# Low halves one step late, pooling products bank by bank, a traced background budget and results held in PSUM, in a two-layer encoder trunk

## The chip, the cores and the metric

The program runs on one core of one Trainium2 chip. The time is the device time of one execution in microseconds (us), from the host's measurement; the profile's span is the time from the first to the last instruction of one profiled execution. TensorE is called PE in the rows (PEld is its weight load), VectorE DVE, ScalarE ACT, GpSimd POOL and SyncE SP. SP issues nearly all loads.

## What is computed

Two post-norm layers over 256 tokens of width 1024, batch 1, all in float32. The part that matters, cut from the reference:

```python
proj = jnp.einsum('bsd,de->bse', x, w_in[i])          # 1024 -> 13824
(a_in, q_att, k_att, v_att, q_h, i_h, ff_h, fb_h, g_h, gate_raw) = jnp.split(proj, splits, axis=-1)
y_a = einsum(multiscale_pool(a_in, pool_w[i], pool_scale[i]), w_branch_a[i])
y_b = einsum(dilated_attention_mixer(q_att, k_att, v_att), w_branch_b[i])
y_c = einsum(hgrn2_bidirectional(q_h, i_h, ff_h, fb_h, g_h, ...), w_branch_c[i])
merged = gates[:, :, 0] * y_a + gates[:, :, 1] * y_b + gates[:, :, 2] * y_c
x1 = layer_norm(DEEPNORM_ALPHA * x + einsum(merged, w_out[i]), ...)
ffn = einsum(silu(einsum(x1, w_ffn_gate[i])) * einsum(x1, w_ffn_up[i]), w_ffn_down[i])
ple = einsum(p[i], w_ple_proj[i]) * sigmoid(einsum(x1, w_ple_gate[i]))
x = layer_norm(DEEPNORM_ALPHA * x1 + ffn + ple, ...)
```

`multiscale_pool` takes centred window means of four channel groups and multiplies each group of 256 channels by its own 256 x 256 matrix `pool_w` (the "pooling products"). HGRN is a gated linear recurrence, run forward and backward over 8 heads of 128, in blocks of time.

## The kernel before

**Weights in chunks.** All weights are read as 214 chunks of 1 MB, in the fixed order in which they are used (the list `chunks`, from L129). SP loads a chunk into a tile `raw`; ScalarE rounds it to its high half `whi` (L212); VectorE subtracts to get the low half `wlo` (L215) and then lets SP load the next chunk into a free `raw` tile. Activations are split in the same way, so a product is three matmuls: high by high, low by high, high by low (`mm3`, L320 to L322; `tok_part`, L369; `gemm_wide` for the FFN, L342). Each of `raw`, `whi`, `wlo` has three buffers, so a chunk can be split as soon as the products of the chunk three places earlier are done. `split_chunk` (L220) issues both halves of the next chunk; `split_later` issues the high half and returns the low half for the caller to place.

**Steps.** The main line is a row of steps, one for each chunk. Within a step TensorE multiplies the chunk into a PSUM bank (`gbank`, four of them, rows named g; `tbank`, four more, rows named t). A chunk of 256 columns (`gemm_cols`) is 48 matmuls of 256 columns; a chunk of the token-major kind (`tok_block`) is 24 matmuls of 512. At the end `step_end` (L309) first runs background work, then evacuates the bank (`then`), then calls `split_chunk`.

**Background.** HGRN (four tasks of two heads), attention (four tasks) and pooling (four tasks) run as Python generators that issue instructions in small pieces and yield the nanoseconds of VectorE time of each. `background` (L268) resumes them until a budget of 3000 is used up. A task that needs TensorE yields None and sleeps until `amid` (L262), which the main line calls in the middle of a chunk, lets it issue its small matmuls there. An HGRN task prepares, for each of two directions, decayed tiles in SBUF (rows named w: scans L486 to L494, reciprocals L499 and L501, products L503 to L539), then issues the products within blocks (the "diagonal", L552), with the second direction also those across blocks (L562, L569), copies them out and goes on to the output (L597 to L625). The tiles that feed the tasks (`half2k`, rows named h) are ten; `room` (L278) forces background work until enough are free. `live` counts the t banks in use and `held` the h tiles.

**Order.** The code sets the order on TensorE, VectorE and ScalarE itself (`manual_schedule`); each engine works through its instructions in that order. A row whose operands carry a wait stops all that stands behind it on that engine.

**Pooling products (from L996).** For each of the four groups one t bank is taken; for m = 0 and 1 the half m of the bank is multiplied (6 matmuls) and split at once into `ph` and `pl_` (L1009, which calls L389 on ScalarE and L390 on VectorE).

**Start and joints.** A few warming matmuls run while the first loads arrive (`spin`, L803), and the first chunk is split in four pieces. Where a layer norm passes the residual stream to the next products (`Handover`) the main line is written out by hand, with single `split_chunk` calls between parts of a chunk; the gate of the per-layer embedding (L1122, L1123 evacuate it) is such a place.

Of the kernel before, what the change touches and what calls it, by code (L numbers as in the profile page):

```python
# [78 lines left out]
def trunk(ctx: ExitStack, tc: tile.TileContext, x, p, w_in, pool_w, pool_scale, w_branch_a,  # L79
# [21 lines left out]
    def misc(shape, dt=F32):  # L101
        return tp.tile(shape, dt, tag="m", bufs=4, name="m")

# [36 lines left out]
    for l in range(DEPTH):  # L140
# [93 lines left out]
    def use_chunk():  # L234
        i = pos["use"]
        pos["use"] += 1
        return split.pop(i)
# [7 lines left out]
    asleep = set()  # L245
    gated = set()
    live = [0]
# [14 lines left out]
    def amid(width=3):  # L262
# [5 lines left out]
    def background(budget=3000, width=3):  # L268
        turn = 0
        while budget > 0:  # L270
# [5 lines left out]
            budget -= resume(t) or 0  # L276
# [32 lines left out]
    def step_end(then=None):  # L309


        background()
        if then is not None:
            then()
# [57 lines left out]
    def tok_block(act, evac, n=2):  # L372

        ps = [gbank(), gbank()]
        for i in range(n):
# [5 lines left out]
            step_end((lambda: [evac(t, ps[t]) for t in range(2)]) if i == n - 1 else None)  # L381
# [82 lines left out]
    def hgrn_task(l, hp, q, ff, kf, fb, kb, vt, gt, oh, ol):  # L464
# [4 lines left out]
        dg, across = None, []  # L469
# [9 lines left out]
        for d in range(2):  # L479
# [5 lines left out]
            if fwd:  # L485
                V.tensor_tensor_scan(out=Ct, data0=smask, data1=f0, initial=0.0, op0=ALU.max, op1=ALU.mult)  # L486
                yield 600
                V.tensor_tensor_scan(out=Rt[:, ::-1], data0=ft[:, 2:514][:, ::-1], data1=emask[:, ::-1],
                                     initial=0.0, op0=ALU.mult, op1=ALU.max)
            else:  # L490
                V.tensor_tensor_scan(out=Ct[:, ::-1], data0=emask[:, ::-1], data1=f0[:, ::-1],
                                     initial=0.0, op0=ALU.max, op1=ALU.mult)
                yield 600
                V.tensor_tensor_scan(out=Rt, data0=ft[:, 0:512], data1=smask, initial=0.0,  # L494
                                     op0=ALU.mult, op1=ALU.max)
            yield 600
# [3 lines left out]
            yield 1670  # L500
            V.reciprocal(out=k2[:, :, la, :], in_=C[:, :, la, :])  # L501
            yield 1670
# [15 lines left out]
            for L, blks, src, intra, own, far, fac in (  # L518
# [3 lines left out]
                for h in range(2):  # L522
                    b0 = blks[0]
                    cs = slice(h * S + 64 * b0, h * S + 64 * b0 + 192)
                    dst = L[:, h, 0:5:2, :].rearrange("p b (c u) -> p b c u", u=32)

                    def v(a):
                        return a[:, cs].rearrange("p (b c u) -> p b c u", c=2, u=32)
                    V.tensor_tensor(out=dst[:, :, own, :], in0=v(src)[:, :, own, :],
                                    in1=v(fac)[:, :, own, :], op=ALU.mult)  # L530
                    V.tensor_tensor(out=dst[:, :, far, :], in0=v(intra)[:, :, far, :],
                                    in1=tot[:, h, b0:b0 + 3, own, :].to_broadcast([P, 3, 32]), op=ALU.mult)
# [693 lines left out]
```

## Time and profile before

| what | value |
|---|---|
| runs, us | 1340.67, 1342.22, 3315.57; median 1342.22 |
| the profiled execution, us | 1341.88 |
| its span, us | 1339.6 |
| its mean granted TensorE clock | 0.983 |
| instructions in the span | 18867 |
| bytes read from HBM | 231.10 MB, 173 GB/s |

The span lies 2.3 us under the execution's own time. In the rows, a group's columns are busy time, mean ns of one, and the idle time of the engine before it with what ended it; a row of the waits gives total time, number and longest wait; a row of the timeline gives start, length, engine, line, operation, tiles and, in brackets, idle time of the engine before it and what ended it. The lengths of matmuls overlap, since they are pipelined: the pace is read from the starts.

The slices of the page, each a fortieth of the span, tenths of busy time and of granted clock:

```profile
PE   9999999999979999999999999999998999999997
DVE  5789897485536866665578999964745468666655
ACT  5444445454434455444254444454533344555541
PEclk9999999999979999999999999999999899999999
```

TensorE falls below 90% in the twelfth slice, with its clock, in the thirty-first, after which its clock falls, and in the last.

### The profile page before, as it was taken

To read this page: it belongs to the slowest core of one execution; us is meant where nothing else is said; L and a number is where in the kernel's file an instruction comes from. 1 tells how busy PE (TensorE), PEld (TensorE's weight loads), DVE (VectorE), ACT (ScalarE), POOL (GpSimd) and SP (SyncE) were. 2 spreads that over 40 slices of the span, in tenths; PEclk is the share of its full clock that TensorE was granted. 3 is DMA by queue.
4 is the path that set the end of the run, shared out by engine and by line. 5 is a ranking of instruction groups with operands and counts; after the bars stand their busy time and mean duration, and the time that the engine had idled before them with its cause. 6 is when DMAs were issued, how large, how long until landed. Compare 5 with 4: busy or idle time off the path is not lost.

```text
span 1339.6 us, 18867 instructions
## 1 busy us (share of the span) xinstructions
PE 1305.8 (97%) x7889; PEld 1152.9 (86%) x7889; DVE 907.6 (68%) x1233; ACT 615.0 (46%) x734; POOL 16.7 (1%) x24
## 2 busy tenths in 40 slices
PE   9999999999979999999999999999998999999997
PEld 7999999998868888888888998999987788888885
DVE  5789897485536866665578999964745468666655
ACT  5444445454434455444254444454533344555541
POOL 0000000000000000000000000000000000000000
PEclk9999999999979999999999999999999899999999
DMA  9555444445545475557555554444366364655570
GB/s 313 185 183 164 158 137 148 142 142 189 188 134 194 145 227 187 172 178 251 187 189 186 161 179 137 131 154 158 126 207 206 102 216 157 191 187 187 176 265 33
DMA packets 160292, 233.36 MB, mean 174 GB/s; under 512 B 3856, under 2 KB 108880, under 8 KB 160208
## 3 DMA queue, kind: packets, MB, share of 16 engines
q1 hardware_dynamic: 158512, 227.44, 51.5%
q10 hardware_dynamic: 1696, 4.72, 1.0%
q8 instruction: 62, 1.02, 0.3%
q14 instruction: 22, 0.18, 0.0%
HBM read 231.10 MB, written 1.05 MB: 173 GB/s over the span
## 4 chain that ended last, share of the span: by engine, by line
PE 74%; DVE 12%; ACT 8%; issue 5%; ACTq 0%; DVEq 0%
PE g L369 32%; PE g L320 11%; PE g L321 11%; PE g L322 11%; ACT whi L212 7%; DVE wlo L215 6%; DVE m L349 2%; DVE m L1163 1%; PE g L342 1%; PE t L569 1%; PE t L320 1%; PE t L552 1%; PE t L645 1%; PE t L408 1%; PE t L598 1%
## 5 line engine op out<-in xcount | busy, mean ns | idle before, releaser
L215 DVE TENSOR_TENSOR wlo<-raw,whi 128x2048 fp32r<-128x2048 f32 (+1 forms) x220 | 489.4, 2229 | 315.3 <-ACT whi L212 315.2
L212 ACT ACTIVATE whi<-raw 128x2048 fp32r<-128x2048 f32 (+1 forms) x220 | 409.2, 1864 | 178.3 <-PE g L369 107.3
L369 PE MATMUL g<-whi,xx 128*128 128x512 f32 x960 | 295.9, 395 | 1.1 <-ACT whi L212 0.8
L320 PE MATMUL g<-xx,whi 128*128 128x256 f32 x896 | 256.8, 287 | 0.0
L321 PE MATMUL g<-xx,whi 128*128 128x256 f32 x896 | 253.9, 283 | 0.0
L322 PE MATMUL g<-xx,wlo 128*128 128x256 f32 x896 | 253.7, 283 | 0.0
L369 PEld LDWEIGHTS g<-whi,xx 128*128 128x128 f32 x960 | 180.3, 191 | 38.0 <-ACT whi L212 2.2
L369 PE MATMUL g<-wlo,xx 128*128 128x512 f32 x480 | 182.7, 393 | 0.2
L320 PEld LDWEIGHTS g<-xx,whi 128*128 128x128 f32 x896 | 172.3, 192 | 0.7
L321 PEld LDWEIGHTS g<-xx,whi 128*128 128x128 f32 x896 | 172.3, 192 | 0.3
L322 PEld LDWEIGHTS g<-xx,wlo 128*128 128x128 f32 x896 | 172.2, 192 | 0.0
L342 PE MATMUL t<-xx,whi 128*128 128x512 f32 x352 | 123.6, 396 | 0.0
L342 PE MATMUL g<-xx,whi 128*128 128x512 f32 x352 | 123.6, 396 | 0.0
L369 PEld LDWEIGHTS g<-wlo,xx 128*128 128x128 f32 x480 | 91.3, 190 | 20.9 <-DVE wlo L215 1.8
L342 PE MATMUL g<-xx,wlo 128*128 128x256 f32 x352 | 91.0, 279 | 0.0
L342 PE MATMUL t<-xx,wlo 128*128 128x256 f32 x352 | 90.9, 279 | 0.0
L342 PEld LDWEIGHTS g<-xx,whi 128*128 128x128 f32 x352 | 64.5, 188 | 12.0
L342 PEld LDWEIGHTS t<-xx,whi 128*128 128x128 f32 x352 | 64.5, 188 | 11.9
L342 PEld LDWEIGHTS t<-xx,wlo 128*128 128x128 f32 x352 | 66.4, 189 | 3.9
L342 PEld LDWEIGHTS g<-xx,wlo 128*128 128x128 f32 x352 | 66.4, 189 | 3.9
L369 PE MATMUL g<-whi,s 128*128 128x512 f32 x192 | 59.1, 389 | 0.0
L320 PE MATMUL g<-whi,s 128*128 128x512 f32 x128 | 50.1, 392 | 0.0
(192 smaller groups left out, 1625.3 us busy)
## 6 DMA issues: line engine op xcount, KB each, us to landing
raw<-in_w_in_dram SPq DMA_DIRECT2D x106, 1024.0 KB, 5.1
raw<-in_w_ffn_gate_dram SPq DMA_DIRECT2D x22, 1024.0 KB, 5.4
raw<-in_w_ffn_up_dram SPq DMA_DIRECT2D x22, 1024.0 KB, 5.4
raw<-in_w_ffn_down_dram SPq DMA_DIRECT2D x22, 1024.0 KB, 5.0
raw<-in_w_branch_c_dram SPq DMA_DIRECT2D x8, 1024.0 KB, 5.2
raw<-in_w_branch_a_dram SPq DMA_DIRECT2D x8, 1024.0 KB, 5.1
raw<-in_w_out_dram SPq DMA_DIRECT2D x8, 1024.0 KB, 4.9
raw<-in_w_ple_gate_dram SPq DMA_DIRECT2D x8, 1024.0 KB, 5.1
```

What stands on the lines that cost most here:

```text
L212: A.activation(out=hi[:, ks, :], in_=t[:, ks, :], func=AF.Copy)
L215: V.tensor_tensor(out=lo[:, ks, :], in0=t[:, ks, :], in1=f(hi[:, ks, :]), op=ALU.subtract)
L320: PE.matmul(ps, lhsT=ah, rhs=bh, start=first, stop=False)
L321: PE.matmul(ps, lhsT=ah, rhs=bl, start=False, stop=False)
L322: PE.matmul(ps, lhsT=al, rhs=bh, start=False, stop=last)
L342: PE.matmul(o, lhsT=a, rhs=b, start=k == 0 and i == 0, stop=k == KD - 1 and i == 1, skip_group_check=True)
L349: V.tensor_tensor(out=dst[:, m, :], in0=dst[:, m, :], in1=ps[m][:, S:2 * S], op=ALU.add)
L369: PE.matmul(ps, lhsT=a, rhs=b, start=i == 0 and k == 0 and p == 0, stop=i == n - 1 and k == 3 and p == 2)
L408: PE.transpose(ps[:, k * P:(k + 1) * P], xt[:, t, (4 * hf + k) * P:(4 * hf + k + 1) * P], ident)
L552: PE.matmul(dg[po:po + 64, co:co + 64], lhsT=KI[:, cs], rhs=QI[:, cs], start=True, stop=True)
L569: PE.matmul(lg[:, co:co + P], lhsT=kp.rearrange("p b u -> p (b u)"), rhs=qp.rearrange("p b u -> p (b u)"), start=True, stop=True)
L598: PE.matmul(o, lhsT=al[:, 2 * h + 1 - t, :], rhs=vt[:, 1 - t, hs], start=False, stop=True)
```

## The change

What it does, part by part:

- `split_chunk` issues the low half of the chunk split one step earlier, and then the high half of the next chunk. `use_chunk` issues an outstanding low half first, if that chunk is used now.
- The pooling products multiply both halves of a bank and then split both.
- The costs that tasks yield are set anew (scans 600 to 1200, reciprocals 1670 to 1730, and others), and what a call of `background` overspends is kept as a debt (`credit`). The attention's steps get a budget of 3300, and four tasks instead of three take turns.
- `step_end` may leave results in their banks (`pend`) while too few h tiles are free, up to `keep` banks, instead of forcing background work by `room` ahead of the product. Tiles are taken at evacuation.
- In HGRN, the diagonal of the first direction is queued for the next `amid` instead of putting the task to sleep; the four operations of 96 elements a side become two of 192; five h tiles are given back at an earlier place. HGRN's and attention's scratch tiles (`misc`) are taken in pairs (`pair`), and some are used twice instead of taking new ones.
- The last value projection of the attention (chunks of `C_VA + 1024`) is used after head pair 3 instead of head pair 2.
- At the start, two warming matmuls instead of three, and the fourth piece of the first chunk is split ahead of the transposed input.

```diff
+    def pair():
+
+        while not all(ring[-4:-2]):
+            yield None
+        ring.extend((False, False))
+        return len(ring) - 2, [tp.tile([P, 512], F32, tag="m", bufs=4, name="m") for _ in range(2)]
...
-        for hp, c0s in enumerate(((C_GH, C_GH + 512), (C_VA, C_VA + 512), (C_VA + 1024,), ())):
+        for hp, c0s in enumerate(((C_GH, C_GH + 512), (C_VA, C_VA + 512), (), (C_VA + 1024,))):
...
+    late = []
+
+    def flush():
+
+        if late:
+            late.pop()()
+
     def split_chunk():
-        i = pos["split"]
-        if i >= NCH:
-            return
-        k, hi_part, lo_part = split_begin()
-        hi_part(slice(0, k))
-        lo_part(slice(0, k))
+
+        flush()
+        if pos["split"] < NCH:
+            late.append(split_later())
...
     def use_chunk():
+        if pos["use"] == pos["split"] - 1:
+            flush()
...
-    def amid(width=3):
+    def amid(width=4):
+        while queued and live[0] < 4:
+            queued.pop(0)()
...
-    def background(budget=3000, width=3):
+    def background(budget=3000, width=4):
         turn = 0
-        while budget > 0:
+        credit[0] = min(credit[0] + budget, max(budget, 3000))
+        while credit[0] > 0:
...
-            budget -= resume(t) or 0
+            credit[0] -= resume(t) or 0
...
-    def step_end(then=None):
-
-
-        background()
+
+    pend = []
+
+    def step_end(then=None, budget=3000, banks=1, need=0, keep=2):
+
+
+        background(budget)
         if then is not None:
-            then()
+            pend.append((then, banks, need))
+        while pend:
+            fn, _, n = pend[0]
+            if held[0] + n > 10 and sum(e[1] for e in pend) <= keep:
+                break
+            pend.pop(0)
+            if n:
+                room(n)
+            fn()
         split_chunk()
...
-            spin(3)
+            spin(2)
...
             piece(2)
+            piece(3)
             split_x(1, 0, turned)
-            piece(3)
...
                     mm3(ps[:, m * S:(m + 1) * S], (w[0][:, 2 * g + k, ms], w[1][:, 2 * g + k, ms]),
                         (mh[:, k, :], ml[:, k, :]), k == 0, k == 1)
+            for m in range(2):
                 i = 2 * g + m
                 if m == 1:
                     held[0] -= 2
...
                 step_end()
+            flush()
             a, b = (n - 2, use_chunk()), (n - 1, use_chunk())
```

How it moves instructions at three places. Line numbers differ between the two kernels: L320, L321, L322 become L356, L357, L358; L215 becomes L228. Tiles s_ with a number are the fixed slots of SBUF.

TensorE at the pooling products of layer 0, before: the first bank's two halves and the start of the second bank, with the engines that a row waits for in brackets.

```order
L320 MATMUL t<-h,whi 128x256 [waits Activation_49]
L321 MATMUL t<-h,whi 128x256
L322 MATMUL t<-h,wlo 128x256 [waits DVE_49]
L320 MATMUL t<-h,whi 128x256
L321 MATMUL t<-h,whi 128x256
L322 MATMUL t<-h,wlo 128x256
L320 MATMUL t<-h,whi 128x256 [waits DVE_49]
```

The same seven rows of TensorE after the change.

```order
L356 MATMUL t<-h,whi 128x256 [waits Activation_49]
L357 MATMUL t<-h,whi 128x256
L358 MATMUL t<-h,wlo 128x256 [waits DVE_49]
L356 MATMUL t<-h,whi 128x256
L357 MATMUL t<-h,whi 128x256
L358 MATMUL t<-h,wlo 128x256
L356 MATMUL t<-h,whi 128x256
```

The matmuls stand as they did; the wait at the head of the second half is gone.

VectorE in layer 0 where head pair 2 of HGRN ends its second direction and head pair 3 begins, before: the last 12 of the 22 rows that stand between two low halves.

```order
L531 TENSOR_TENSOR w<-w,tot 128x3x32
L529 TENSOR_TENSOR w<-h,w 128x3x32
L531 TENSOR_TENSOR w<-w,tot 128x3x32
L535 TENSOR_TENSOR t_1748<-tot 128x8
L539 TENSOR_TENSOR w<-w,t_1748 128x2x64 x2
L575 COPY_PREDICATED attF<-kc,t 128x256
L486 SCALAR_TENSOR_TENSOR w<-kc,h 128x512
L575 COPY_PREDICATED attB<-kc,t 128x256
L488 SCALAR_TENSOR_TENSOR w<-h,kc 128x512
L584 TENSOR_TENSOR m<-attF,attB 64x4x64 x2
L499 RECIPROCAL w<-w 128x8x32
L501 RECIPROCAL w<-w 128x8x32
```

The same work of VectorE after the change.

```order
L563 TENSOR_TENSOR w<-h,w 128x2x3x32
L565 TENSOR_TENSOR w<-w,tot 128x2x3x32
L569 TENSOR_TENSOR t_1828<-tot 128x8
L573 TENSOR_TENSOR w<-w,t_1828 128x2x64 x2
L228 TENSOR_TENSOR wlo<-raw,whi 128x2048
L620 COPY_PREDICATED attF<-kc,t 128x256
L522 SCALAR_TENSOR_TENSOR w<-kc,h 128x512
L620 COPY_PREDICATED attB<-kc,t 128x256
L524 SCALAR_TENSOR_TENSOR w<-h,kc 128x512
L628 TENSOR_TENSOR m<-attF,attB 64x4x64 x2
L535 RECIPROCAL w<-w 128x8x32
L228 TENSOR_TENSOR wlo<-raw,whi 128x2048
```

The one long run is cut by low halves: the tiles that the diagonal needs are ready ahead of one, and its copies stand behind it. On TensorE this diagonal stood between two chunks; now it stands in the middle of the chunk three further on.

VectorE at the gate of the layer's embedding in layer 0, before: two low halves, the evacuation of the first bank, a low half.

```order
L215 TENSOR_TENSOR wlo<-raw,whi 128x2048
L417 TENSOR_TENSOR xx<-t,xx 128x4x128 x2
L215 TENSOR_TENSOR wlo<-raw,whi 128x2048 x2
L1122 SCALAR_TENSOR_TENSOR m<-m,s_4112 128x512
L1123 SCALAR_TENSOR_TENSOR x<-x,m 128x512
L215 TENSOR_TENSOR wlo<-raw,whi 128x2048
```

VectorE at the same place after the change.

```order
L228 TENSOR_TENSOR wlo<-raw,whi 128x2048
L453 TENSOR_TENSOR xx<-t,xx 128x4x128 x2
L228 TENSOR_TENSOR wlo<-raw,whi 128x2048
L1167 SCALAR_TENSOR_TENSOR m<-m,s_4067 128x512
L1168 SCALAR_TENSOR_TENSOR x<-x,m 128x512
L228 TENSOR_TENSOR wlo<-raw,whi 128x2048
```

The low half of the next chunk to be used has moved from ahead of the evacuation to behind it.

More of the change, by code (lines that the diff above doesn't have):

```diff
@@ L380, in tok_block @@
                     amid()
-            step_end((lambda: [evac(t, ps[t]) for t in range(2)]) if i == n - 1 else None)
+            step_end((lambda: [evac(t, ps[t]) for t in range(2)]) if i == n - 1 else None, banks=2)
     def split_to(hi, lo, src, scale=None):
@@ L521, in hgrn_task, with v @@
                     L = KL = work([P, 2, 5, 64])
[L522 to L532, printed above, removed]
-                    yield 400
+                b0 = blks[0]
+                dst = L[:, :, 0:5:2, :].rearrange("p h b (c u) -> p h b c u", u=32)
+                def v(a):
+                    return c4(a)[:, :, b0:b0 + 3]
+                V.tensor_tensor(out=dst[:, :, :, own, :], in0=v(src)[:, :, :, own, :],
+                                in1=v(fac)[:, :, :, own, :], op=ALU.mult)
+                V.tensor_tensor(out=dst[:, :, :, far, :], in0=v(intra)[:, :, :, far, :],
+                                in1=tot[:, :, b0:b0 + 3, own, :].to_broadcast([P, 2, 3, 32]), op=ALU.mult)
+                yield 600
             t64 = small([P, 2, 4, 1], "t64")
@@ L540, in hgrn_task, with diagonal @@
                                 in1=t64[:, :, sc, :].to_broadcast([P, 2, 64]), op=ALU.mult)
-            yield 500
-            yield None
-            if dg is None:
-                yield from banks_for(1)
-                dg = tbank()
-            else:
+            held[0] -= 5 * d
+            yield 650
+            def diagonal(d=d, KI=KI, QI=QI):
+                if d == 0:
+                    live[0] += 1
+                    dgs.append(tbank())
+                for h in range(2):
+                    for b in range(4):
+                        cs = slice(h * S + 64 * b, h * S + 64 * b + 64)
+                        po, co = 64 * (b % 2), d * S + (2 * h + b // 2) * 64
+                        PE.matmul(dgs[0][po:po + 64, co:co + 64], lhsT=KI[:, cs], rhs=QI[:, cs],
+                                  start=True, stop=True)
+            if d == 0:
+                queued.append(diagonal)
+            else:
+                yield None
+                while not dgs:
+                    yield None
                 yield from banks_for(2)
-            for h in range(2):
-                for b in range(4):
-                    cs = slice(h * S + 64 * b, h * S + 64 * b + 64)
-                    po, co = 64 * (b % 2), d * S + (2 * h + b // 2) * 64
-                    PE.matmul(dg[po:po + 64, co:co + 64], lhsT=KI[:, cs], rhs=QI[:, cs], start=True, stop=True)
+                at_ring, both_ = yield from pair()
+                diagonal()
             across.append((QL, KL))
@@ L572, in hgrn_task @@
                 busy.clear()
-                held[0] -= 5
+        dg = dgs[0]
         for d, t, k in ((0, F, K_TRIF), (1, B, K_TRIB)):
@@ L577, in hgrn_task @@
             yield 330
-        at = misc([P, 4, P])
-        al = misc([P, 4, P])
+        at, al = (a.rearrange("p (g c) -> p g c", c=P) for a in both_)
         for hf in range(2):
@@ L639, in attn_task @@
         yield None
+        sc_ring, scs = yield from pair()
         yield from banks_for(2)
@@ L919, in ev @@
                         V.tensor_tensor(out=gt[:, t, 512 * hf:512 * hf + 512], in0=ps, in1=s, op=ALU.mult)
+                        if hf == 1 and t == 1:
+                            gated.add(l)
                     tok_block(xtok, ev)
-                gated.add(l)
-            for g in {1: (0, 1), 2: (2,)}.get(hp, ()):
-                def ev(t, ps):
+            for g in {1: (0, 1), 3: (2,)}.get(hp, ()):
+                def ev(t, ps, g=g):
                     dst = va[:, t, 512 * g:512 * g + 512] if g < 2 else vb[:, t, :]
```

87 lines of the change are left out of this document (45 added, 42 removed).

## The prediction

> **What bounds the kernel now.** I read the page first, then its slices, then who waits on TensorE, then each stretch in which TensorE idles or loses clock.
>
> ```profile
> PE 1305.8 (97%) x7889; PEld 1152.9 (86%) x7889; DVE 907.6 (68%) x1233; ACT 615.0 (46%) x734; POOL 16.7 (1%) x24
> L215 DVE TENSOR_TENSOR wlo<-raw,whi 128x2048 fp32r<-128x2048 f32 (+1 forms) x220 | 489.4, 2229 | 315.3 <-ACT whi L212 315.2
> ```
>
> TensorE is busy 97% of 1339.6 us. VectorE is busy 68%, and 315.2 us of its idle time is the low half of a chunk (wlo) waiting for the high half (whi) just issued on ScalarE. That wait is off the path as long as TensorE has work, so the question is where TensorE has none. Its own waits:
>
> ```profile
> PE t L320 <- DVE s L390: 14.3, 8, 3.9
> PE t L552 <- DVE w L507: 5.7, 2, 3.5
> ```
>
> Eight waits in the pooling products, two before the diagonal products of HGRN; nothing else reaches 2 us. Stretches cut at the first matmul of chunks (columns: stretch, length, busy time and count by engine, granted clock, DMA share, GB/s): three undisturbed ones, then the pooling chunk with the chunk behind it, per layer, then the two chunks around the late diagonal, per layer, then the end of the FFN's hidden part, per layer.
>
> ```profile
> 37.86:43.62 5.76, 5.76 (x50) 5.76 (x49) 3.94 (x8) 3.38 (x3) 0.00 (x0) 1.00 0.53 181
> 346.18:351.62 5.44, 5.44 (x26) 4.50 (x24) 2.81 (x2) 2.43 (x3) 0.00 (x0) 1.00 0.57 191
> 83.52:98.81 15.29, 15.29 (x131) 14.15 (x129) 9.76 (x14) 8.31 (x18) 1.03 (x1) 1.00 0.58 191
> 367.94:386.21 18.27, 11.12 (x50) 10.02 (x48) 7.55 (x12) 5.20 (x8) 0.00 (x0) 0.60 0.40 130
> 386.21:392.81 6.60, 6.60 (x25) 5.34 (x25) 2.78 (x2) 2.27 (x2) 0.00 (x0) 0.82 0.08 12
> 1029.68:1047.95 18.27, 11.11 (x49) 10.01 (x48) 7.57 (x12) 5.20 (x8) 0.00 (x0) 0.61 0.41 130
> 1047.95:1054.77 6.82, 6.82 (x25) 5.50 (x25) 2.78 (x2) 2.27 (x2) 0.00 (x0) 0.79 0.12 18
> 167.83:179.81 11.98, 9.49 (x90) 9.04 (x89) 11.91 (x25) 3.64 (x5) 0.00 (x0) 0.88 0.52 174
> 179.81:187.67 7.86, 7.86 (x66) 7.86 (x66) 7.33 (x7) 4.09 (x12) 0.41 (x1) 0.96 0.01 2
> 827.90:841.17 13.27, 9.47 (x92) 8.99 (x91) 13.16 (x29) 3.64 (x5) 0.00 (x0) 0.92 0.49 158
> 841.17:849.40 8.23, 8.23 (x66) 8.23 (x66) 7.57 (x8) 4.09 (x12) 0.48 (x1) 0.92 0.01 2
> 607.30:624.50 17.20, 16.79 (x73) 13.29 (x72) 11.87 (x11) 9.14 (x8) 0.00 (x0) 1.00 0.75 270
> 1269.30:1286.50 17.20, 16.77 (x74) 13.31 (x72) 11.84 (x11) 9.14 (x8) 0.00 (x0) 1.00 0.77 267
> ```
>
> An undisturbed chunk of 48 matmuls takes 5.76 us, one of 24 takes 5.44. The kernel is bound by TensorE's work, plus these few holes and the low clock that follows them.
>
> **Pooling products, bank by bank.** Column half m=1 of a bank waits until VectorE has read half m=0 out of the same bank:
>
> ```profile
> 368.53 0.29 PE L322 MATMUL t<-h,wlo 128*128 128x256 f32 x1
> 372.72 0.58 PE L320 MATMUL t<-h,whi 128*128 128x256 f32 x1 [3.90 <-DVE s L390]
> 376.73 0.58 PE L320 MATMUL t<-h,whi 128*128 128x256 f32 x1 [1.08 <-DVE s L390]
> ```
>
> After the change both halves are multiplied first, and the order shows no wait of TensorE on VectorE between them; the next group writes another bank. The chunk then needs 5.76 us, and the one behind it 5.44 at full clock. Saved: (18.27 - 5.76) + (6.60 - 5.44) = 13.67 us in layer 0, and (18.27 - 5.76) + (6.82 - 5.44) = 13.89 us in layer 1; 27.56 in all. The eight evacuations are not gone: 8 x 0.48 us on VectorE now end about 2 us behind the products, and their reader comes two chunks (10.9 us) later. Next late there would be the low half behind them, some 2 us ahead of its reader.
>
> **HGRN's diagonal products.** The task of head pair 3 needs tiles that head pair 2 holds, so room() pushes all of pair 2's second direction into VectorE's queue between two low halves, and puts the diagonal directly behind the chunk on TensorE:
>
> ```profile
> 166.60 1.22 DVE L491 TENSOR_TENSOR_SCAN w<-kc,h 128x512 f32<-128x512 f32 x1
> 172.26 2.28 DVE L215 TENSOR_TENSOR wlo<-raw,whi 128x2048 fp32r<-128x2048 f32 x1
> 175.47 0.42 DVE L507 TENSOR_TENSOR w<-h,w 128x256 f32<-128x256 f32 x1
> 175.94 0.69 PE L552 MATMUL t<-w 128*64 128x64 f32 x16 [2.19 <-DVE w L507]
> ```
>
> Now results wait in PSUM instead (pend), and in the new order that diagonal stands in the middle of a chunk, half a chunk (2.9 us) behind the point at which its last VectorE operation is due, with a low half and not a new task's scans in between. The stretch 83.52 to 98.81 holds the same small products around two chunks of 24, so without a hole two chunks of 48 would take 15.29 + 2 x 0.32 = 15.93 us. Saved: 11.98 + 7.86 - 15.93 = 3.91 us, and 13.27 + 8.23 - 15.93 = 5.57; 9.48 in all. If VectorE lags by more than those 2.9 us the wait comes back.
>
> The low clock is in both sums. TensorE waited 2.19 us in layer 0 and the clock fell to 0.88 over that stretch and 0.96 over the next. [...]
>
> **Low half one step behind.** VectorE's low half no longer stands directly behind its high half, so VectorE stops waiting for ScalarE. That is worth nothing by itself while TensorE is fed, except where VectorE and ScalarE hand over to each other and fall behind, as in the FFN, whose lead is used up at its end:
>
> ```profile
> 619.16 0.50 PE L321 MATMUL g<-wlo,sb 128*128 128x512 f32 x1 [0.41 <-DVE wlo L215]
> ```
>
> Idle there 17.20 - 16.79 = 0.41 and 0.43; 0.84 saved. The price is lead: where VectorE must evacuate a bank between, the low half now comes a step later. In the FFN the second product's evacuation is the longest:
>
> ```profile
> 490.07 0.38 ACT L348 ACTIVATE m<-g 128x256 f32<-128x256 f32 x1 [2.39 <-PE g L342]
> 490.49 0.42 DVE L349 TENSOR_TENSOR m<-m,g 128x256 f32<-128x256 f32 x1 [0.95 <-ACT m L348]
> 497.23 0.69 DVE L1163 TENSOR_TENSOR m<-m 128x512 f32<-128x512 f32 x1
> 497.96 0.63 ACT L386 ACTIVATE sa<-m 128x512 fp32r<-128x512 f32 x1 [1.91 <-DVE m L1163]
> 498.62 0.69 DVE L387 TENSOR_TENSOR sa<-m,sa 128x512 fp32r<-128x512 f32 x1 [0.70 <-ACT sa L386]
> ```
>
> 0.38 + 0.42 + 0.69 + 0.63 + 0.69 + 2.29 for the low half = 5.1 us after the product ends, and TensorE wants it one chunk (about 5.6 us) later: it fits by 0.5. In the HGRN stage a step holds 3 us of background (the new budget, in traced durations), one or two of the evacuations below, and 2.29:
>
> ```profile
> L919 DVE TENSOR_TENSOR s<-g,m 128x512 f32<-128x512 f32 x8 | 5.0, 667 | 0.0
> L889 DVE TENSOR_TENSOR h<-h,g 128x512 f32<-128x512 f32 x8 | 5.3, 668 | 2.2 <-ACT h L888 2.2
> ```
>
> That is 3.0 + 0.67 + 2.29 = 5.96 us against chunks of 5.76, or 6.6 against 5.44, with HGRN's own products lengthening every second or third chunk (15.29 - 2 x 5.44 = 4.41 us for one such set) and some steps without evacuation. VectorE keeps up on average, with 1.5 to 2 us in hand at the tightest steps. I take 0, with bounds of 0 and 1 us in each of 16 steps. The raw load is released later with it; ScalarE then may wait, but its high halves lead by a step more than the low ones.
>
> One place loses for certain. In the gate of the layer's embedding the low half of the next chunk stood ahead of an evacuation and now stands behind it:
>
> ```profile
> 472.24 0.69 DVE L1123 SCALAR_TENSOR_TENSOR x<-x,m 128x512 f32<-128x512 f32 x1
> 473.86 0.39 PE L369 MATMUL g<-wlo,xx 128*128 128x512 f32 x1
> ```
>
> It can start at 472.24 + 0.69 = 472.9 and ends at 475.2, while TensorE reads it at 473.86: 1.3 us, in each layer, 2.6. Whether such a wait halves the clock for one window, as 2.19 us did and 0.41 us did not (row 619.16; clock 1.00 over that stretch, 607.30), no row tells. Half a window of 3.4 us would add 1.7 each. 1.3 is a little nearer to 0.41; I take no drop and keep 3.4 for the range.
>
> **Start, yields, merged operations.** One warming matmul is dropped and the fourth piece's high half goes ahead of a transpose's evacuation:
>
> ```profile
> 1.45 2.93 PE L805 MATMUL t<-w 128*128 128x256 f32 x6 [1.45 <-DVE w L801]
> 7.69 0.63 ACT L212 ACTIVATE whi<-raw 128x512 fp32r<-128x512 f32 x1 [0.79 <-DMA raw<-in_w_in_dram]
> 10.08 0.73 PE L369 MATMUL g<-whi,xx 128*128 128x512 f32 x2 [0.47 <-ACT whi L212]
> ```
>
> The swap removes the 0.47 us wait. The warming matmul's 0.4 (2.93 / 6, less overlap) is taken back by the load on which ScalarE waits at 7.69. I take 0.5, between 0 and 0.9. Four 96-element operations become two of 192, on VectorE only: it eases the lag and costs the path nothing. The exchanged weight chunks (value projection of the attention) move as a pair with their transfers, and the held results take banks that TensorE needs four steps later: 0 each.
>
> **Sum.** Against the profiled execution, 1341.88 us (0.34 under the median of the runs shown, which I neglect): -27.56 - 9.48 - 0.84 - 0.5 + 2.6 = -35.8, so 1306 us, 2.7% faster. All new waits absent: 1303.5. With both half-clock windows: 1309.5.
>
> **Rivals.**
> - Lateness in the HGRN stage. For it: VectorE is the busiest helper there, 13.16 of 13.27 us in the layer 1 row, and each low half loses a step of lead. Against it: the forced burst is gone and so is its waiting for whi. At 1 us in each of 16 steps it gives 1306 + 16 = 1322 us, within 2%.
> - The wait on VectorE in the pooling products stays in another form, as a wait for a bank or for a late low half: 27.56 is not gained, 1334 us. Against it: the stretch before has no other user of these banks.
> - Slower: the lag repeats itself at every chunk of the HGRN and attention stages, because a step's VectorE work exceeds a chunk. From 35.8 / 58 = 0.62 us a chunk (29 chunks a layer) the gain is eaten; at 1 us a chunk it gives 1306 + 58 = 1364 us. Against it: in the attention stage VectorE has slack, and the order shows 3 to 4 us of background a step.
>
> **How the numbers follow.** 0.69 for the forecast with its own range of 1303 to 1310, 0.17 for lateness in HGRN, 0.08 for pooling unchanged, 0.06 for slower. A difference under 2%, which is about what a measurement of this kernel can tell from none, ends at 1315.4. Faster by more: 0.69 plus the mild third of the lateness, 0.75. Within: 0.19. Slower: 0.06. The range that leaves 2 in 10 out runs from 1301 to 1320: it takes in the forecast and most of the lateness.
>
> **What would show it.** Right: no row of TensorE waiting on VectorE in the pooling products and that chunk at about 5.8 us at clock 1.00; no wait before a diagonal; VectorE's idle time before wlo, 315 us, mostly gone; a wait of about 1.3 us on wlo in each layer's embedding gate; TensorE busy about 99%. Wrong: waits of TensorE on wlo spread over the HGRN stage, a second low-clock stretch, or a pooling chunk far over 6 us.

## The result, and the profile after

| | before | after |
|---|---|---|
| median of the runs, us | 1341.72 | 1304.11 (1303.77 to 1304.44) |
| ratio, 95% interval | | 0.9722 [0.9703, 0.9741] |
| profiled execution, its span, us | 1341.88, 1339.6 | 1304.44, 1302.7 |
| mean granted TensorE clock | 0.983 | 0.998 |

One of the four runs of the kernel before took 3315.57 us and is left out of the ratio. The change makes the kernel 2.8% faster; 1306 us was predicted, with a range of 1301 to 1320. The rows of the page after the change that answer to those of before (engines, the low half's group, two rows of slices):

```profile
PE 1288.0 (99%) x7887; PEld 1137.9 (87%) x7887; DVE 901.3 (69%) x1169; ACT 620.0 (48%) x734; POOL 16.7 (1%) x24
PE   9999999999999999999999999999999999999997
PEclk9999999999999999999999999999999999999999
L228 DVE TENSOR_TENSOR wlo<-raw,whi 128x2048 fp32r<-128x2048 f32 (+1 forms) x220 | 487.8, 2225 | 88.4 <-ACT whi L225 88.2
```

TensorE's share went from 97% to 99%, both dips of busy time and clock are gone, and the low half's waiting for the high half fell from 315.2 to 88.2 us. That last number, the largest that the change moves, bought nothing on the whole, as the experiments show. What TensorE still waits for after the change (total, times, longest; one more of 0.2 us follows):

```profile
PE g L405 <- DVE wlo L228: 2.3, 2, 1.2
PE t L850 <- DVE w L846: 1.5, 1, 1.5
PE g L405 <- ACT whi L225: 0.7, 2, 0.3
```

The eight waits of the pooling products and the two of HGRN have left the list. Two on a low half are new. The stretches of the pooling chunk and the one behind it, and of the last three chunks of the FFN's hidden part, cut as in the prediction:

```profile
362.86:368.52 5.66, 5.66 (x50) 5.66 (x48) 4.81 (x6) 3.21 (x4) 0.00 (x0) 1.00 0.24 55
368.52:373.97 5.45, 5.45 (x26) 4.51 (x25) 3.82 (x7) 3.96 (x6) 0.00 (x0) 1.00 0.48 186
590.27:606.59 16.32, 16.32 (x73) 13.51 (x72) 10.79 (x7) 6.67 (x5) 0.00 (x0) 1.00 0.86 308
1005.61:1011.32 5.71, 5.71 (x50) 5.71 (x48) 4.85 (x6) 3.20 (x4) 0.00 (x0) 1.00 0.26 58
1011.32:1016.77 5.45, 5.45 (x26) 4.51 (x25) 3.83 (x6) 3.96 (x6) 0.00 (x0) 1.00 0.48 182
1233.07:1249.39 16.32, 16.32 (x73) 13.51 (x72) 10.79 (x7) 6.67 (x5) 0.00 (x0) 1.00 0.86 307
```

18.27 us became 5.66 and 5.71, at clock 1.00, and TensorE is busy in all of every stretch. These starts against the same starts before give an account of the whole gain by place:

| place | how read | predicted | measured |
|---|---|---|---|
| start, HGRN and attention, layer 0 | 367.94 - 362.86 | 0.5 + 3.91 | 5.08 |
| pooling, layer 0 | (18.27 + 6.60) - (5.66 + 5.45) | 13.67 | 13.76 |
| behind pooling up to the FFN's last chunks, layer 0 | (607.30 - 590.27) - (392.81 - 373.97) | -1.3 | -1.81 |
| FFN's end, layer 0 | 17.20 - 16.32 | 0.41 | 0.88 |
| HGRN and attention, layer 1 | (1029.68 - 1005.61) - (624.50 - 606.59) | 5.57 | 6.16 |
| pooling, layer 1 | (18.27 + 6.82) - (5.71 + 5.45) | 13.89 | 13.93 |
| behind pooling, layer 1 | (1269.30 - 1233.07) - (1054.77 - 1016.77) | -1.3 | -1.77 |
| FFN's end, layer 1 | 17.20 - 16.32 | 0.43 | 0.88 |

They add up to 37.11 us; the last stretches and what lies outside the span add 0.33, since 1341.88 - 1304.44 = 37.44.

### The profile page after: what moved, and what is told of

It reads as the page before. It is cut to its first block, busy times and chain, and to the rows that moved or that the text cites. A ratio compares the mean times of both kernels' runs of the same rounds, so it can differ in the third digit from the quotient of the medians.

```text
span 1302.7 us, 18708 instructions
## 1 busy us (share of the span) xinstructions
PE 1288.0 (99%) x7887; PEld 1137.9 (87%) x7887; DVE 901.3 (69%) x1169; ACT 620.0 (48%) x734; POOL 16.7 (1%) x24
## 4 chain that ended last, share of the span: by engine, by line
PE 96%; DVE 2%; DMA 0%; ACT 0%; issue 0%; SPq 0%; DVEq 0%
PE g L405 32%; PE g L356 13%; PE g L358 13%; PE g L357 13%; PE t L378 9%; PE g L378 9%; DVE wlo L228 1%; PE t L587 1%; PE t L614 1%; PE t L642 1%; PE t L641 1%; PE t L721 1%; PE t L690 1%; PE t L444 0%; DMA raw<-in_w_in_dram 0%; PE t L669 0%
## 5 line engine op out<-in xcount | busy, mean ns | idle before, releaser
L228 DVE TENSOR_TENSOR wlo<-raw,whi 128x2048 fp32r<-128x2048 f32 (+1 forms) x220 | 487.8, 2225 | 88.4 <-ACT whi L225 88.2
L356 PE MATMUL g<-xx,whi 128*128 128x256 f32 x896 | 255.8, 285 | 0.0
L358 PE MATMUL g<-xx,wlo 128*128 128x256 f32 x896 | 253.5, 283 | 0.0
L357 PE MATMUL g<-xx,whi 128*128 128x256 f32 x896 | 253.4, 283 | 0.0
L356 PEld LDWEIGHTS g<-xx,whi 128*128 128x128 f32 x896 | 171.8, 192 | 0.6
L357 PEld LDWEIGHTS g<-xx,whi 128*128 128x128 f32 x896 | 171.9, 192 | 0.3
L358 PEld LDWEIGHTS g<-xx,wlo 128*128 128x128 f32 x896 | 171.8, 192 | 0.0
L405 PE MATMUL g<-whi,s 128*128 128x512 f32 x192 | 59.1, 389 | 0.0
L385 DVE TENSOR_TENSOR m<-m,t 128x256 f32<-128x256 f32 x44 | 18.5, 421 | 56.1 <-ACT m L384 56.1
```

The source lines that it names most:

```text
L228: V.tensor_tensor(out=lo[:, ks, :], in0=t[:, ks, :], in1=f(hi[:, ks, :]), op=ALU.subtract)
L356: PE.matmul(ps, lhsT=ah, rhs=bh, start=first, stop=False)
L357: PE.matmul(ps, lhsT=ah, rhs=bl, start=False, stop=False)
L358: PE.matmul(ps, lhsT=al, rhs=bh, start=False, stop=last)
L385: V.tensor_tensor(out=dst[:, m, :], in0=dst[:, m, :], in1=ps[m][:, S:2 * S], op=ALU.add)
L405: PE.matmul(ps, lhsT=a, rhs=b, start=i == 0 and k == 0 and p == 0, stop=i == n - 1 and k == 3 and p == 2)
```

## The experiments

Each number is a median of four runs (five for the last); "the kernel before" ran on the same chip. Ratios are to the kernel before, with their 95% intervals. The changed kernel was not run again beside them, so a difference to it, or between two experiments, can be one between two chips; where it is under 3 us it is read together with the rows of the traces.

### Pooling products alone, and everything but them

The kernel before with one line more, so that both halves are multiplied and then both are split:

```diff
                     mm3(ps[:, m * S:(m + 1) * S], (w[0][:, 2 * g + k, ms], w[1][:, 2 * g + k, ms]),
                         (mh[:, k, :], ml[:, k, :]), k == 0, k == 1)
+            for m in range(2):
                 i = 2 * g + m
```

> The kernel before with one edit: both halves of a pooling bank are multiplied before both are split; all else as before. My theory: TensorE's wait on VectorE and the half clock behind it go, in both layers, worth 27.6 us: 1314 us, and the pooling chunk takes 5.8 us at clock 1.00. Rival 1: with the low halves and the background as before, VectorE is late at that place (the first wait was 3.9 us, not 1.1) and part of the wait moves to the next chunk's low half: 1318 to 1325 us. Rival 2: the pooling part is worth little by itself and the gain comes from the whole: over 1330 us.

Measured: 1314.24 us (1313.82 to 1315.14), ratio 0.9797 [0.9782, 0.9812]. That is 1341.5 - 1314.24 = 27.3 us against the predicted 27.56. Of the two large waits on VectorE only HGRN's is left in its list (no other there exceeds 1.5 us):

```profile
PE t L552 <- DVE w L507: 5.7, 2, 3.5
```

The reverse, the changed kernel without that line:

> The changed kernel with the pooling products as before (each half of a bank split before the other half is multiplied). My theory: the parts add up, so it is 27.6 us slower than the changed kernel, 1331.7 us, with eight waits of TensorE on VectorE and 17 us of half clock a layer. Rival: VectorE, which no longer waits for the high halves, reads the banks sooner, so the first wait of 3.9 us shrinks to the 1.1 us of the others: about 22 us slower, 1326 us.

Measured: 1322.11 us (1320.92 to 1329.86), ratio 0.9867 [0.9838, 0.9896]: 18.0 us over the changed kernel and not 27.6. One execution of the four took 1329.86 us, at a mean clock of 0.985; the others took 1320.92 to 1322.84, at 0.993 to 0.996. All eight waits are there, almost as long as before the change: 13.4 us in all, the longest 3.5 (`PE t L356 <- DVE s L426` in its list), against 14.3 and 3.9.

So the holes are nearly the same in both, and what follows the holes is not. Before, the half clock lasted 17.07 us in each layer (0.50 over 371.52 to 388.58 and 1033.70 to 1050.77); here it lasted 3.41 us (0.50 over 366.03 to 369.44 in layer 0). That called for a run on the clock itself: the same kernel, with the gate's low half moved ahead as in a run below.

> The pooling products multiplied and split half by half as before the change, everything else as changed, and the low half ahead of the first evacuation in the embedding's gate. The same eight holes of TensorE in each execution. Theory (the granted clock is decided for fixed windows of 3.413 us, whose phase differs from run to run, and is given back only after a window with little idle time): executions fall into two groups or more, near 1322.1 - 2.7 = 1319.4 us at a mean clock of 0.993 to 0.996 and near 1327 us at about 0.985, and the profile's stretch of half clock is a whole number of windows. Rival (the holes alone set the clock): all executions within 1 us of 1319.4.

Measured: 1322.33 us (1321.39 to 1322.56), ratio 0.9858 [0.9844, 0.9873], all at a mean clock of 0.990 to 0.992. The theory's two groups did not appear; all executions lay between them. The profile shows why, cut at the steps of the granted clock and every 3.41 us from them (layer 0 up to 386.27, layer 1 from 1017.74):

```profile
362.38:365.79 3.41, 1.09 (x8) 0.84 (x6) 2.89 (x3) 2.39 (x2) 0.00 (x0) 1.00 0.06 16
365.79:369.21 3.42, 2.28 (x10) 2.28 (x11) 1.17 (x3) 0.47 (x1) 0.00 (x0) 0.50 0.56 159
369.21:372.62 3.41, 2.33 (x12) 2.03 (x11) 0.88 (x2) 0.47 (x1) 0.00 (x0) 0.50 0.56 214
...
379.45:382.86 3.41, 3.41 (x12) 2.93 (x12) 1.70 (x2) 2.21 (x2) 0.00 (x0) 0.50 0.00 0
382.86:386.27 3.41, 3.41 (x16) 2.75 (x16) 3.19 (x2) 0.07 (x1) 0.00 (x0) 1.00 0.36 68
1017.74:1021.15 3.41, 0.03 (x1) 0.03 (x1) 3.30 (x4) 1.41 (x2) 0.00 (x0) 1.00 0.25 77
1021.15:1024.57 3.42, 2.91 (x12) 2.61 (x12) 0.48 (x1) 0.95 (x2) 0.00 (x0) 0.50 0.77 253
1024.57:1027.98 3.41, 1.75 (x13) 1.56 (x13) 1.45 (x3) 0.95 (x2) 0.00 (x0) 1.00 0.14 54
1027.98:1031.39 3.41, 2.33 (x18) 2.12 (x19) 0.97 (x2) 0.95 (x2) 0.00 (x0) 1.00 0.02 5
```

The same pooling edit makes four holes in each layer of one execution, yet layer 0 stays at half clock for five windows (365.79 to 382.86) and layer 1 for one. The steps to half clock lie on one grid of these windows: (1021.15 - 365.79) / 192 = 3.4133, and (1033.70 - 371.52) / 194 = 3.4133 in the kernel before. Counted from the first instruction the grid stands at 0.6 us here (365.79 - 107 x 3.4133) and at 2.9 in the kernel before (371.52 - 108 x 3.4133). In layer 0 the first half-clock window is busy for 2.28 us, and the next is at half clock again; in layer 1 it is busy for 2.91 us, and the clock comes back. There the window behind it, at full clock and busy for 1.75 us, is followed by another at full clock. The two layers differ in where the grid falls on the holes. The pooling part is therefore worth 27.3 us from the kernel before, and 18.0 to 20.9 (1322.33 against 1301.41, below) when taken back from this one, for the same edit.

### The low half at once, and the gate

The changed kernel with each low half directly behind its high half:

```diff
-        flush()
         if pos["split"] < NCH:
-            late.append(split_later())
+            split_later()()
```

> The changed kernel, but each chunk's low half is issued right behind its high half, as before; background, held results, pooling and start stay changed. My theory: where TensorE is fed the place of the low half is worth nothing; the two waits of 1.33 us at the embedding gate go, the two holes of 0.4 us at the end of the FFN's hidden part come back: 1304.1 - 2.7 + 0.8 = 1302.2 us. Rival: VectorE waits for ScalarE again (315 us before, 88 us after), falls behind in the HGRN stage, and TensorE waits there: 1308 us or more.

Measured: 1302.44 us (1302.17 to 1302.75), ratio 0.9708 [0.9692, 0.9724]. Taking out the lateness makes the changed kernel 1.7 us faster: the two gate waits go, and the two at the FFN's end come back (0.9 us in its list of waits). A third place shows only in the starts. Behind the evacuations of the pooling products three low halves follow each other on VectorE in the changed kernel, and a weight load waits for the first of them:

```profile
371.94 0.48 DVE L426 SCALAR_TENSOR_TENSOR s<-t,vec,s 128x256 fp32r<-128x256 f32 x1 [0.54 <-ACT s L425]
372.35 6.69 DVE L228 TENSOR_TENSOR wlo<-raw,whi 128x2048 fp32r<-128x2048 f32 x3
374.68 0.19 PEld L405 LDWEIGHTS g<-wlo,xx 128*128 128x128 f32 x1 [0.52 <-DVE wlo L228]
```

The chunk takes 5.83 us (373.97 to 379.80), and 5.82 in layer 1 (1016.77 to 1022.59), where the kernel before (392.81 to 398.25) took 5.44; with the low half at once it takes 5.44 again (373.95 to 379.39). By the starts the sum is then 2 x 1.33 (derived at the next run) + 0.39 + 0.38 - 2 x 0.88 = 1.67 us. Next, the lateness kept, with the outstanding low half put ahead of the gate's first evacuation:

```diff
         split_chunk()
+        flush()
         go(0, 1, (2,))
         ev(0, 0, ps[0])
```

> The changed kernel, but at the embedding gate the outstanding low half is issued ahead of the first bank's evacuation. My theory: the wait of 1.33 us on wlo goes in both layers and nothing takes its place: 1304.1 - 2.7 = 1301.4 us. Rival: the evacuation behind it is late instead and the wait comes back one chunk later: 1304 us.

Measured: 1301.41 us (1300.49 to 1301.79), ratio 0.97 [0.9685, 0.9714]: 2.7 us less than the changed kernel, for two waits of 1.17 us each in the matmul rows. From start to start each is 1.33: the matmuls ahead start every 0.23 us, the last at 455.10, and the waiting one starts at 456.66 (its row is shown with the account of the prediction) and not at 455.33.

### Holding results, and counting in traced durations

The changed kernel with nothing held in PSUM:

```diff
-    def step_end(then=None, budget=3000, banks=1, need=0, keep=2):
+    def step_end(then=None, budget=3000, banks=1, need=0, keep=0):
...
-                step_end(ev_qk, 3300, need=1, keep=3)
+                step_end(ev_qk, 3300, need=1)
```

> The changed kernel with results never held in PSUM: a result that finds no free tile forces background work at once, as before; the traced durations stay. Theory (the forced burst of VectorE work made the hole before the late diagonal products of HGRN, and holding removed it): by the order, some 5 us of VectorE work of head pair 2 then stands again between two low halves and the diagonal one chunk earlier on TensorE, so a wait of TensorE on VectorE of 2 to 4 us returns in each layer, with a half-clock window: 1304.1 + 4 to 9, 1310 us. Rival (the traced durations in the budget did it, since less is left over to be forced): no wait on VectorE before the diagonal, 1303 to 1305 us.

Measured: 1327.05 us (1326.37 to 1327.76), ratio 0.9897 [0.988, 0.9913], 22.9 us over the changed kernel. Both theories missed it: the price is far larger, and the wait is another one. From its list of waits, and from its timelines of VectorE and TensorE in layer 0:

```profile
PE g L358 <- DVE wlo L228: 15.6, 4, 4.8
...
172.48 1.21 DVE L530 TENSOR_TENSOR_SCAN w<-h,kc 128x512 f32<-128x512 f32 x1
...
180.05 4.49 DVE L228 TENSOR_TENSOR wlo<-raw,whi 128x2048 fp32r<-128x2048 f32 x2
...
182.39 0.39 PE L358 MATMUL g<-xx,wlo 128*128 128x256 f32 x1 [3.02 <-DVE wlo L228]
```

The forced burst, 172.48 to 180.05, stands ahead of a low half that TensorE needs in the chunk under way. The trace has four windows of half clock besides (221.69, 836.09 and two from 873.63, each 3.41 us; the mean clock is 0.992); with up to half of that, 1.7 us, lost in each, 15.6 + 4 x 1.7 = 22.4 us is most of the 22.9. Then the changed kernel with the old counting:

```diff
-                yield 1200
+                yield 600
...
-        credit[0] = min(credit[0] + budget, max(budget, 3000))
-        while credit[0] > 0:
+        while budget > 0:
...
-                step_end(ev_qk, 3300, need=1, keep=3)
+                step_end(ev_qk, need=1, keep=3)
```

(the other costs in the same way: reciprocals 1670, merged products 800, 500 and 660).

> The changed kernel with the old counting of background: 600 ns declared for a scan that takes 1.22 us, nothing carried from step to step, 3000 a step in attention; results still held in PSUM. Theory (holding removed the hole; the counting only keeps a step short): the second directions are made earlier, no tile is missing, no wait before a diagonal; a step may hold 4.5 to 5 us of background, which with 0.67 and 2.29 is 7.6 to 8 us against chunks of 5.76, so some low halves come 1 to 2 us late: 1304 to 1309, point 1306. Rival (the counting was what removed the hole): waits before the diagonals as before the change, 1311 to 1314 us.

Measured: 1325.55 us (1325.18 to 1325.79), ratio 0.9883 [0.9869, 0.9898], 21.4 us over the changed kernel, and again neither theory. Its list of waits and one such step in its timelines:

```profile
PE g L404 <- DVE wlo L228: 8.8, 9, 2.0
PE g L357 <- DVE wlo L228: 7.3, 9, 1.4
...
717.03 1.22 DVE L526 TENSOR_TENSOR_SCAN w<-kc,h 128x512 f32<-128x512 f32 x1
718.17 1.20 DVE L529 TENSOR_TENSOR_SCAN w<-h,kc 128x512 f32<-128x512 f32 x1
719.40 1.75 DVE L534 RECIPROCAL w<-w 128x256 f32<-128x256 f32 x1
721.07 1.70 DVE L536 RECIPROCAL w<-w 128x256 f32<-128x256 f32 x1
722.68 2.23 DVE L228 TENSOR_TENSOR wlo<-raw,whi 128x2048 fp32r<-128x2048 f32 x1
...
724.97 0.39 PE L357 MATMUL g<-xx,wlo 128*128 128x256 f32 x1 [1.43 <-DVE wlo L228]
```

A step that is charged 600 + 600 + 1670 + 1670 ns holds 5.65 us of work by its starts (717.03 to 722.68); with the low half of 2.23 it is longer than the chunk of 5.76 us beside it. This is the lateness that the prediction had as a rival, in 16 places beside the two gate waits. The matmul rows put those 16 at 13.8 us, too little for 21.4. The weight loads, which can wait where the matmul behind them shows no wait (0.52 us at 374.68, above), have 26.1 us in 30 places (15.8 at L404, 10.3 at L357), against 6.1 us in 9 in the changed kernel: 20.0 more, and with 1.7 for the one window of half clock (0.50 over 824.04 to 827.46) the 21.4 is accounted for.

In both runs the victim is a late low half. So the same two edits were made on the kernel with the low half at once.

> The changed kernel with results never held in PSUM and each low half issued at once behind its high half. Theory (holding is needed because the low half is late: a burst of 7.4 us on VectorE, forced by a missing tile, then stands ahead of a low half that TensorE reads in the chunk under way): at once the low half is a step of 5.76 us earlier, the waits on wlo of 3 and 4.8 us go, and what returns is at most the wait of the diagonal products that the kernel before had: 1302.4 + 2 to 9, point 1308. Rival (the burst costs the same wherever the low half stands): 1322 to 1327 us.

Measured: 1302.30 us (1302.21 to 1302.57), ratio 0.9731 [0.9709, 0.9752]; with holding it was 1302.44. No row of TensorE waiting for a diagonal is in its list. Holding is worth 22.9 us with the late low half and nothing without it.

> The changed kernel with the old counting of background and each low half issued at once behind its high half. Theory (counting by traced durations is needed because the low half is late): the 18 waits on wlo, 16 us in all, go, since each low half has a step more in hand: 1302.4 to 1306, point 1303.5. Rival (too much background in a step makes low halves late wherever they stand): 1315 to 1325 us.

Measured: 1307.37 us (1305.72 to 1308.87), ratio 0.9768 [0.974, 0.9795]: all but 4.9 of the 21.4 us go, as the theory says, though it ends above its range. In its list all waits on low halves in HGRN are gone; one among the products across blocks, in layer 1, is new:

```profile
PE t L605 <- DVE w L563: 2.4, 1, 2.4
```

It brings one window of half clock (a stretch across its edge, 813.80 to 817.20, shows 0.77). Counting by traced durations is worth 4.9 us without the lateness and 21.4 with it.

### What removed the HGRN hole

If neither holding nor, mostly, counting removed it, the candidate left was the count of free tiles. In the changed kernel five tiles are given back before the diagonal; put back behind the products, in the kernel with the low half at once and nothing held:

```diff
-            held[0] -= 5 * d
             yield 650
...
             if d == 1:
                 busy.clear()
+                held[0] -= 5
```

> The kernel of the run before (low half at once, nothing held) with one line put back: the five tiles of a head pair count as free only behind the diagonal and cross products, not as soon as VectorE has made their operands. Theory (in the kernel before, it was this count that put the diagonal directly behind the forced burst; freed early, it runs half a chunk later with 2 us in hand): a wait of TensorE on VectorE before or among the diagonal products comes back, with a half-clock window: 1302.3 + 2 to 9, point 1308. Rival (the place of room(), now at the evacuation and not ahead of the chunk, did it): no wait, 1302 to 1303.5.

Measured: 1319.80 us (1318.75 to 1321.12), ratio 0.9852 [0.9825, 0.9879]: 17.5 us more, twice the upper end of the expected. From its list of waits:

```profile
PE t L585 <- DVE w L542: 9.2, 4, 3.1
PE t L605 <- DVE w L564: 1.4, 4, 0.4
```

Four waits rather than two, each followed by one window at half clock: 9.2 + 1.4 + 4 x 1.7 = 17.4 us. The mean clock, 0.993 against 0.998 without this edit, fits four: 0.007 x 1318.6 - 0.002 x 1300.6 = 6.6 us. `room` goes on until the count falls, so a count that falls behind the products pulls these up to the burst. Then this edit alone, with the pooling edit, on the kernel before:

```diff
+            held[0] -= 5 * d
             yield 500
...
                 busy.clear()
-                held[0] -= 5
```

> The kernel before the change with two small edits alone: the pooling products multiplied for both halves first, and the five tiles counted as free as soon as VectorE has made their operands. Theory (these two hold all that the change gains on the path, but for the FFN's end and the start): 1314.2 - 9.5 = 1304.8, between 1303 and 1307 us, and no wait before the late diagonal. Rival (the hole in HGRN needs the place of room() or the counting as well): 1311 to 1315.

Measured: 1314.74 us (1313.62 to 1315.49), ratio 0.9816 [0.9785, 0.9847], against 1314.24 without the early release. The theory falls. Head pair 2 of layer 0 has no wait any more, and head pair 3 has one in its place (its list of waits and timeline):

```profile
PE t L553 <- DVE w L507: 6.0, 3, 2.7
...
213.58 0.69 PE L553 MATMUL t<-w 128*64 128x64 f32 x16 [2.71 <-DVE w L507]
```

So the early release is not enough, and without it the hole is there (shown with the low half at once and nothing held; from the changed kernel itself it was not taken back). What keeps the hole from moving on to head pair 3 (`room` called at the evacuation, the queued diagonal, the paired scratch tiles, the exchanged value chunks) was not separated.

### The lateness where it helps

The kernel with the low half at once and nothing held, with the low half late in the FFN alone (`lag` is set where the FFN begins and cleared at its end):

```diff
+        flush()
         if pos["split"] < NCH:
-            split_later()()
+            lo = split_later()
+            late.append(lo) if lag[0] else lo()
```

> The kernel with the low half at once and nothing held (1302.3), with the low half one step late in the FFN alone. Theory (the lateness is worth something only where VectorE and ScalarE hand over to each other, and nothing elsewhere): the two waits at the FFN's end, 0.9 us, go: 1302.3 - 0.9 = 1301.4, as the version with the gate's low half ahead. Rival (a late low half in the FFN brings its own waits, or moves the 0.9 elsewhere): 1302.0 to 1304.

Measured: 1300.43 us (1299.95 to 1300.80), ratio 0.9701 [0.9681, 0.9721], the shortest of all. The gain is 1.9 us, twice the 0.9 expected and close to 2 x 0.88 in the table of places. What TensorE still waits for is the start: 1.4 us once, and two waits of 0.4 us and less.

## Why the prediction held, step by step

- **Pooling products, 27.56.** Right, in mechanism and size: 27.69 by the stretches, 27.3 alone. Nearly half of it, 27.56 less 14.3 us of waits, was the low clock behind the holes, and it was read from this kernel's own rows. Undone from the changed kernel the same edit costs 18.0 to 20.9, since fewer windows of half clock follow the holes there (one in layer 0 of the first run, five and one in the two layers of the second, five in each layer before).
- **HGRN's diagonal products, 9.48.** The places gave 5.08 + 6.16 = 11.24 with the start in it, against 9.98 for these two terms, 1.3 us more than predicted. Half of that is a misreading. The stretch 83.52 to 98.81 does not stand "around two chunks of 24": TensorE's timeline there holds one chunk of 48 (L320 to L322, 16 rows each) and one of 24 (L369), so two chunks of 48 with the same small products take 15.29 + 0.32 = 15.61 us and not 15.93, and the term comes to 10.12. (In the same way the 4.41 us for one set of small products is 4.09.) The remaining 0.6 us was not told apart. The reason was half right. The products do stand clear of their operands after the change, by the timelines of VectorE and TensorE:

```profile
179.98 0.42 DVE L543 TENSOR_TENSOR w<-h,w 128x256 f32<-128x256 f32 x1
...
183.87 0.49 DVE L573 TENSOR_TENSOR w<-w,t 128x128 f32<-128x128 f32 x2
...
187.54 0.69 PE L587 MATMUL t<-w 128*64 128x64 f32 x16
188.06 0.64 PE L607 MATMUL t<-w 128*64 128x64 f32 x16
```

  The diagonal (L587) reads tiles that are ready behind L543, at 180.40, 7.1 us ahead of it. L573 ends the tiles of the products across blocks (L607), 188.06 - (183.87 + 0.49) = 3.7 us ahead of them; the prediction had 2.9 from the order, without keeping the two apart. But "now results wait in PSUM instead" is not why: without holding there was no hole either, at 1302.30 with the low half at once. The late release of the tiles brings the hole back, at 17.5 us; the early release alone only moves it.
- **Low half one step behind.** "Worth nothing by itself" was right, and where it helps the size was low: 0.88 at each FFN's end against 0.41 and 0.43. The prediction took the idle time in the matmul row of the last wait (0.41 at 619.16); the weight load in front of that matmul had waited 0.83 us for the same low half, and that is close to the excess from start to start over the last chunks.
- **The embedding's gate, 2.6.** Right: the low half starts when the first evacuation is through, and TensorE waits for it in each layer.

```profile
453.71 0.69 DVE L1168 SCALAR_TENSOR_TENSOR x<-x,m 128x512 f32<-128x512 f32 x1
454.32 2.29 DVE L228 TENSOR_TENSOR wlo<-raw,whi 128x2048 fp32r<-128x2048 f32 x1
...
456.66 0.50 PE L405 MATMUL g<-wlo,xx 128*128 128x512 f32 x1 [1.17 <-DVE wlo L228]
```

  Removing both waits gave 2.7 us. They did not lower the clock, as taken (1.00 over 5.96 to 1296.20). The 3.4 us kept for the range is half a window at each of two waits; such a window, at half clock for 3.41 us, stands behind HGRN's hole in the kernel before (0.50 over 176.96 to 180.37). The places show 0.5 us a layer more. Of this 0.4 is the late low half behind the pooling products (373.97 to 379.80, above), which the prediction had "some 2 us ahead of its reader". It let the evacuations end about 2 us behind the products; they end at 371.94 + 0.48 = 372.42, 3.9 us behind 368.52, where the next chunk starts.
- **Lateness in HGRN, 0 with bounds of 0 and 16.** Right for this kernel. The upper bound was too low for what can happen: with the old counting it came, at 21.4 us with one window of half clock. The order had shown the new budget holding; it did not show how much hung on it.
- **Start, 0.5.** In this trace the chunk that began at 37.86 begins at 37.50, 0.4 us earlier. The same chunk begins between 36.83 and 37.97 in the other traces read with the new start, and at 38.02 and 38.08 in the two with the old one, so the size is right and the scatter is as large.

The forecast was 1.9 us too high: HGRN with the start 1.3, the FFN's end 0.9, the pooling products 0.1, the end and outside the span 0.3, less 1.0 behind the pooling products, and 0.3 between the profiled execution and the median.

The parts do not add up to the whole. Pooling alone gives 27.3 of 37.6 us. The late low half costs 1.7, and with it in place holding and counting keep the kernel from losing 22.9 and 21.4 us; without it they are worth 0 and 4.9. Someone who undoes each part in turn would rank holding and counting beside the pooling edit, though both mostly repair what the late low half brings. Neither was added alone to the kernel before.

## What to carry to other kernels

Before moving work later, list what stands between its new place and its reader on the in-order engine, because every burst there now delays it: here a move that saved 227 us of VectorE's waiting for ScalarE cost 1.7 us and made two other parts worth over 20 us each. Undo a part in the final kernel and also add it alone to the first; where the two numbers differ, the parts protect each other. When a hole is removed from a place where work is forced by a count of free buffers, look at the next user of these buffers, where the hole may reappear. To price a late weight tile, read the waits of the weight loads and the starts: idle time in the matmul rows came out at 0.41 for 0.88 us, and at none for 0.39.

## What the runs showed of the hardware

The steps of the granted clock lie on one grid within an execution, and not at the start of a hole: in the kernel before half clock begins at 176.96, 371.52, 839.14 and 1033.70, with 57, 137 and 57 times 3.413 us between them, and the first three of these are 3.2, 2.7 and 5.1 us behind the starts of the holes (173.75, 368.82 and 834.03). The rows above have steps to half clock behind windows in which TensorE was busy for 1.09 and 0.03 us, and none behind one busy for 1.75. Busy time alone does not settle it: in the run with pooling and release, two windows of 1.9 us in a row, busier than that, led to half clock in layer 0 and not in layer 1:

```profile
208.95:212.36 3.41, 1.92 (x17) 1.72 (x15) 3.41 (x3) 1.54 (x1) 0.00 (x0) 1.00 0.38 127
212.36:215.78 3.42, 1.90 (x35) 1.68 (x36) 3.38 (x17) 0.29 (x1) 0.00 (x0) 1.00 0.00 0
215.78:219.19 3.41, 3.41 (x18) 3.41 (x18) 3.36 (x5) 1.07 (x3) 0.00 (x0) 0.50 0.07 17
857.48:860.89 3.41, 1.87 (x16) 1.67 (x14) 3.41 (x3) 1.49 (x1) 0.00 (x0) 1.00 0.38 129
860.89:864.31 3.42, 1.95 (x36) 1.73 (x37) 3.38 (x17) 0.34 (x1) 0.00 (x0) 1.00 0.00 0
864.31:867.72 3.41, 3.41 (x31) 3.41 (x30) 3.36 (x5) 1.02 (x3) 0.00 (x0) 1.00 0.08 21
```

On the way back, at half clock, a window busy for 2.28 or 2.33 us was followed by another at half clock, one busy for 2.91 by full clock. So in one execution the four holes of the same edit held TensorE at half clock for five windows in layer 0, and in layer 1, once it was back at full clock behind one window, left it there (1.75 us busy at 1024.57). The clock also splits the runs of the kernel before: beside the experiments it took 1335.0 to 1337.5 us at a mean clock of 0.987 or 0.988, and 1339.7 to 1342.6 at 0.981 to 0.985. Four windows at half clock in one layer would be 4 x 3.41 x 0.5 = 6.8 us of TensorE's time, 0.5% of the span, which is about that difference in clock; whether it is this was not tried. The gains above are against medians that mostly lie in the longer group, as the profiled execution does; against the shorter one, 1336.84 in the same series, the pooling edit alone is worth 22.6 us and not 27.3.
